# A mixture-of-experts kernel whose token rows for the third and later experts are gathered in three steps among the products of the expert before

## The chip, the cores and the metric

One core of one Trainium2 chip runs the whole program. The metric is device time in microseconds (us): the median of three runs. Besides, one execution was recorded by the hardware profiler; all rows below are from that one. A core has TensorE (PE; its weight loads are shown apart as PEld), VectorE (DVE), ScalarE (ACT), GpSimd (POOL), SyncE (SP) and 16 DMA engines. TensorE reads SBUF and writes PSUM; the other engines bring PSUM back into SBUF.

## The reference

One layer of a diffusion backbone on 512 tokens of 1024 columns: a mixer (attention, a Hyena and a convolution group, an output projection), then a mixture of 16 experts in which every expert picks its 64 tokens. All values are float32. What matters here is the second half:

```python
def expert_choice_ffn(h, w_router, w1, w3, w2):
    cap = EC_CAPACITY * L // N_EXPERTS
    aff = jax.nn.softmax((h @ w_router).astype(jnp.float32), axis=-1)
    gate, idx = lax.top_k(jnp.swapaxes(aff, 1, 2), cap)
    xe = h[b_idx, idx]
    a = jnp.einsum('becd,edf->becf', xe, w1)
    u = jnp.einsum('becd,edf->becf', xe, w3)
    y = jnp.einsum('becf,efd->becd', jax.nn.silu(a) * u, w2)
    y = y * gate[..., None].astype(y.dtype)
    return jnp.zeros_like(h).at[b_idx, idx].add(y)
...
h2 = modulate(rmsnorm(x, norm2_g[l]), sh2, sc2)
x = x + g2 * expert_choice_ffn(h2, router_w[l], expert_w1[l], expert_w3[l], expert_w2[l])
return rmsnorm(x, final_norm_g)
```

## The kernel before

The first 400 us hold the mixer and the routing; they end with `idxf`, the list of each expert's 64 token numbers. From there a loop over the 16 experts (line 1267 on) runs, one expert after the other. An expert's weights are 24 tiles of 128 x 2048 float32, 1 MB each: for each k of 8 one tile of w1 and one of w3, then eight tiles of w2. They are loaded by SyncE's queue, in the order of use, into a pool of 22 such tiles (`U`, tag "U"). Two of the 22 hold the running sums (`acc`) from expert 1 on and two the rows of x (`xblk`), so 18 are left for loads, 20 once the rows of x are given back. `take` asks for a loaded tile, `free` gives it back after its last product and issues the next load; each of these waits for the products that read its buffer, and for the load eight places ahead of it to land. A load is thus held up whenever TensorE stands still for long.

The steps of an expert, with their names: for each k, 8 products into four PSUM tiles `pa` (lines 1279 and 1280), with the expert's transposed token rows `xT[:, k, cs]` (64 columns) as the stationary side and the weight tile as the moving side of 512 columns. `xT` is half of the tile `xh` and holds two experts' columns side by side, 64 each. A float32 product shows as two records in the trace, a transpose as one. After every second k one piece of `scatter` of the preceding expert follows: two products `pZ` (line 1177) that add its rows `yg` onto the sums, with additions on VectorE (line 1180). Then VectorE and ScalarE copy `pa` to `au` (lines 103 and 105, in turn), 16 transposes bring it into `pT` (line 1307), ScalarE and VectorE make `hT` of it (1309, 1310), and 32 products `py` (line 1320) with the eight w2 tiles follow. VectorE scales the result into `yg` (line 1324).

The token rows come from `gather(i)`, which serves the two experts 2i and 2i+1 at once. TensorE broadcasts the two lists (`pB`, line 1155), VectorE compares them with the token numbers into `ohg`, one-hot columns times the token's norm factor (line 1159), and for each of eight blocks of columns TensorE multiplies four 128 x 128 blocks of x, as the stationary side, with four blocks of `ohg`, 128 moving columns each (line 1167), so that the result is already transposed. `modulate2` (lines 1060 and 1062, ScalarE and VectorE in turn) takes each block from PSUM into `xT` with scale and shift. `gather(0)` runs among the first products of expert 0. For each odd expert but the last the whole gather for the next two experts stands between its `pa` products and its 16 transposes.

TensorE's order in the loop is the order of the code (`manual_schedule` for PE); the queues of the other engines are set by a scheduler. PSUM tiles come from three pools: "A" (four, `pa`), "T" (two: `pT` and `pZ`) and "Y" (two: `pB`, `pG`, `py`). The last expert's own residual rows are gathered by `final_rows` (line 1225) with one-hot columns as the stationary side.

Of the kernel before, what the change touches and what calls it, by code (L numbers as in the profile page):

```python
# [21 lines left out]
E = 16  # L22
# [28 lines left out]
def hybrid_kernel(ctx: ExitStack, tc: tile.TileContext, a, out: bass.AP):  # L51
# [34 lines left out]
    def psT(name="psT"):  # L86
        return psum.tile([128, 512], FT, name=name, tag="T", bufs=2)
# [682 lines left out]
    def finish(*gens):  # L770
        for g in gens:
            for _ in g:
                pass
# [374 lines left out]
    nc.vector.tensor_tensor(idxf, bc(sel), rv(lf[1])[:, None, :].to_broadcast([16, 2, CAP]), op=OP.add)  # L1148
    nc.vector.tensor_tensor(vals, bc(lv[0]), rv(lv[1])[:, None, :].to_broadcast([16, 2, CAP]), op=OP.max)

    def gather(i):

        pb = psY("pB")
        for s in range(2):
            mm(pb[:, 64 * s:64 * s + 64], ident[0:16, 2 * i + s:2 * i + s + 1].to_broadcast([16, 128]), idxf[:, 0],
               start=True, stop=True)
        g = W("ohg")
        for b in range(4):
            nc.vector.tensor_scalar(g[:, 128 * b:128 * b + 128], pb[:, 0:128], tok[:, b:b + 1], rsT[:, b:b + 1],
                                    op0=OP.is_equal, op1=OP.mult)  # L1160
        yield
        for k in range(8):
            if k % 4 == 0 or i == 0:
                p = psT("pT")
            pk = p[:, (k % 4) * 128:(k % 4 + 1) * 128]
            for b in range(4):
                mm(pk, xblk(b)[:, k * 128:(k + 1) * 128], g[:, b * 128:(b + 1) * 128], start=(b == 0), stop=(b == 3))  # L1167
            modulate2(xT[:, k], pk, k)
            yield

    def scatter(e, yg, oh):

        def block(c):
            ps = [psT("pZ") for _ in range(2)]
            for h in range(2):
                pr = slice(64 * h, 64 * h + 64)
                mm(ps[h], oh[pr, 128 * c:128 * c + 128], yg[pr], start=True, stop=True)  # L1177
            for h in range(2):
                s = slice(512 * h, 512 * h + 512)
                nc.vector.tensor_add(ablk(c)[:, s], (ablk if e else xblk)(c)[:, s], ps[h])  # L1180
        return [lambda c=c: block(c) for c in range(4)]
# [10 lines left out]
    xhU = late.tile([128, 2048], FT, name="xh")  # L1192
    xT = half(xhU, 0).rearrange("p (k n) -> p k n", k=8)
    hT = half(xhU, 1).rearrange("p (f n) -> p f n", f=16)
    first = gather(0)
    in_order = ExitStack()
    in_order.enter_context(tc.manual_schedule(engines={mybir.EngineType.PE}))
    next(first)
# [68 lines left out]
    for e in range(E):  # L1267
# [4 lines left out]
            nc.vector.tensor_scalar(oh, iota, ig[:, e:e + 1], None, op0=OP.is_equal)  # L1272
        pa = [psA("pa") for _ in range(4)]
        back = deque(scatter(*prev)) if prev is not None else deque()
        for k in range(8):
            w1, w3 = take(("w1", e, k)), take(("w3", e, k))
            for f in range(4):
                s = slice(512 * f, 512 * f + 512)
                mm(pa[f][0:64], xT[:, k, cs], w1[:, s], start=(k == 0), stop=(k == 7))  # L1279
                mm(pa[f][64:128], xT[:, k, cs], w3[:, s], start=(k == 0), stop=(k == 7))  # L1280
                if e == 0 and f == 1:
                    next(first, None)
            free(2, 2 if e == 1 and k < 2 else 0)
            if k == 1 and e == 1:
                acc = [U("acc0"), U("acc1")]
            for _ in range(2 if last and k else int(k % 2 == 1)):
                if back:
                    back.popleft()()
            if last and k == 3:
                rows = final_rows()  # L1290
                bg = next(rows)
            if last and k == 5:
                fgh, pairs, where = next(rows)
                next(rows)
        assert not back
        au = [W("au") for _ in range(4)]
        for f in range(4):
            copy(au[f], pa[f])
        if e % 2 == 1 and e + 1 < E:
            finish(gather(e // 2 + 1))  # L1300
            if e + 3 == E:
                free_only(2)
        for f in range(4):
            p = psT("pT")
            for i in range(4):
# [137 lines left out]
```

## Time and profile before

| what | value |
|---|---|
| median of three runs | 1355.02 us (1353.71 to 1356.91) |
| the profiled execution | 1362.26 us, its span 1360.5 us |
| mean granted TensorE clock | 0.955 |
| TensorE busy | 1253.2 us (92%) |
| VectorE, ScalarE, GpSimd busy | 491.1, 213.1, 154.3 us |
| DMA | 458.01 MB, mean 337 GB/s over the span |
| pa products (lines 1279, 1280) | 2048 records, 596 ns each, two at a time |
| py products (line 1320) | 1024 records, 596 ns each, two at a time |
| gather products (line 1167) | 512 records, 363 ns each, 101.9 us busy |

The profile is read in this manner. Busy shares are of one execution, and are averages over stretches with different limits. The slices give the shares over time; windows give them for a stretch between two named moments, with the clock that TensorE was granted (1.00 is 2.4 GHz, 0.50 is 1.2 GHz) and the rate of the DMA engines. The timeline gives instructions in order, with the idle time before them and what ended it; rows of one kind are merged, so the second number is the stretch that all of them took together. What sets the time of a stretch is the wait in it that ends last.

### The profile page before, as it was taken

How to read it: one execution, taken by the hardware profiler on the slowest of the kernel's cores; microseconds unless marked ns; L12 is line 12 of the kernel's file. 1: busy time of each engine (PE TensorE's matmuls, PEld its weight loads, DVE VectorE, ACT ScalarE, POOL GpSimd, SP SyncE). 2: the span in 40 equal slices, each digit the busy share in tenths (PEclk: the TensorE clock that was granted, in tenths of full speed). 3: DMA queues.
4: the chain of work that ended last, by engine and by line, in shares of the span. 5: the costliest groups of instructions: out<-in, count | busy, mean ns of one | idle time of the engine just before them, and what ended most of it. 6: DMA issues, size and time to landing. Idle time of an engine off the chain costs nothing.

```text
span 1360.5 us, 15095 instructions
## 1 busy us (share of the span) xinstructions
PE 1253.2 (92%) x6084; PEld 614.1 (45%) x6084; DVE 491.1 (36%) x971; ACT 213.1 (16%) x445; POOL 154.3 (11%) x166
## 2 busy tenths in 40 slices
PE   5898988899979999998998999899899999989997
PEld 2576567766644344335334333533433353353332
DVE  6877998478580121211112122021211212121224
ACT  3532232245420100001000000000100000000002
POOL 1333444546110000000000000000000000000000
PEclk9998999999989989996999999799999989979998
DMA  9934124634367997999999999999999999999994
GB/s 354 354 135 170 67 66 113 216 136 171 126 247 317 421 422 289 422 421 407 421 422 421 421 420 422 421 422 421 422 420 422 421 421 421 421 421 421 422 421 189
DMA packets 72980, 458.01 MB, mean 337 GB/s; under 512 B 7364, under 2 KB 9228, under 8 KB 21710
## 3 DMA queue, kind: packets, MB, share of 16 engines
q1 hardware_dynamic: 71662, 453.64, 82.2%
q0 software_dynamic: 912, 3.06, 0.9%
q8 instruction: 48, 0.79, 0.2%
q10 hardware_dynamic: 336, 0.35, 0.1%
q14 instruction: 22, 0.18, 0.0%
HBM read 453.87 MB, written 2.36 MB: 335 GB/s over the span
## 4 chain that ended last, share of the span: by engine, by line
PE 65%; DMA 16%; DVE 15%; issue 2%; ACT 2%; POOLq 0%; DVEq 0%; SPq 0%; ACTq 0%
PE pa L1279 24%; DMA ld<-in_w_dram 15%; PE py L1320 12%; PE pT L1167 7%; DVE glu L590 4%; PE pZ L1177 4%; PE pT L1307 2%; PE pP L550 1%; PE pP L548 1%; PE pP L549 1%; PE pS L932 1%; PE pO L963 1%; PE pM L431 1%; PE pX L548 1%; PE pX L550 1%
## 5 line engine op out<-in xcount | busy, mean ns | idle before, releaser
L1280 PE MATMUL pa<-ld,xh 128*64 128x512 f32 x1024 | 455.9, 596 | 3.3 <-DMA ld<-in_w_dram 3.3
L1279 PE MATMUL pa<-ld,xh 128*64 128x512 f32 x1024 | 455.6, 596 | 0.3 <-DVE xh L1062 0.3
L1279 PEld LDWEIGHTS pa<-ld,xh 128*64 128x64 f32 x1024 | 135.7, 137 | 280.0 <-issue 267.9
L1320 PE MATMUL py<-ld,xh 128*64 128x512 f32 x1024 | 224.4, 596 | 0.0
L1180 DVE TENSOR_TENSOR acc<-acc,pZ 128x512 f32<-128x512 f32 x112 | 72.0, 684 | 296.7 <-PE pZ L1177 296.7
L1280 PEld LDWEIGHTS pa<-ld,xh 128*64 128x64 f32 x1024 | 135.6, 137 | 20.4 <-issue 12.9
L1320 PEld LDWEIGHTS py<-ld,xh 128*64 128x64 f32 x1024 | 72.3, 137 | 140.1 <-issue 135.5
L1167 PE MATMUL pT<-ohg,ld 128*128 128x128 f32 x512 | 101.9, 363 | 31.1 <-DVE xh L1062 15.1
L103 ACT ACTIVATE au<-pa 128x512 f32<-128x512 f32 x32 | 19.1, 597 | 632.3 <-PE pa L1280 632.3
L1167 PEld LDWEIGHTS pT<-ohg,ld 128*128 128x128 f32 x512 | 87.8, 257 | 49.6 <-DVE xh L1062 22.1
L1347 POOL DMA_INDIRECT out_dram<-yg,where x1 | 1.1, 1096 | 950.9 <-DVE yg L1346 950.9
L1324 DVE SCALAR_TENSOR_TENSOR yg<-py,ig,g1bc 128x512 f32<-128x512 f32 x16 | 12.0, 752 | 206.1 <-PE py L1320 206.1
L516 POOL TENSOR_TENSOR wl<-ld,wh 128x512 fp32r<-128x512 f32 x44 | 64.5, 1492 | 85.8 <-ACT wh L515 46.3
L1177 PE MATMUL pZ<-yg,oh 64*128 64x512 f32 x240 | 68.9, 641 | 1.5 <-DVE acc L1180 1.5
L548 PE MATMUL pP<-hh,wh 128*128 128x512 f32 x144 | 58.8, 409 | 1.2 <-ACT hh L505 1.2
L550 PE MATMUL pP<-hh,wl 128*128 128x512 f32 x144 | 57.2, 405 | 2.7 <-DVE wl L516 2.7
L549 PE MATMUL pP<-hl,wh 128*128 128x512 f32 x144 | 57.0, 397 | 1.5 <-DVE hl L507 1.5
L590 DVE SCALAR_TENSOR_TENSOR glu<-glu,p 128x512 f32<-128x512 f32 x60 | 56.9, 949 | 1.1
L1307 PE MATMUL pT<-c,au 128*128 128x128 f32 x256 | 46.0, 315 | 11.4 <-DVE acc L1180 5.4
L1062 DVE TENSOR_SCALAR xh<-pT,A,B 128x128 f32<-128x128 f32 x32 | 13.1, 410 | 112.1 <-PE pT L1167 112.1
L105 DVE COPY au<-pa 128x512 f32<-128x512 f32 x32 | 22.1, 692 | 74.1 <-PE pa L1280 72.0
L1307 PEld LDWEIGHTS pT<-c,au 128*128 128x128 f32 x256 | 36.9, 209 | 25.7 <-DVE acc L1180 11.2
(336 smaller groups left out, 1279.0 us busy)
## 6 DMA issues: line engine op xcount, KB each, us to landing
ld<-in_w_dram SPq DMA_DIRECT2D x384, 1024.0 KB, 19.8
ld<-in_w_mod_dram SPq DMA_DIRECT2D x24, 1024.0 KB, 13.5
ld<-in_w_in_dram SPq DMA_DIRECT2D x11, 1024.0 KB, 5.2
ld<-in_w_out_dram SPq DMA_DIRECT2D x4, 1024.0 KB, 5.3
ld<-in_x_dram SPq DMA_DIRECT2D x2, 1024.0 KB, 12.0
ld<-in_x_dram SPq DMA_DIRECT2D x4, 512.0 KB, 6.7
out_dram<-acc SPq DMA_DIRECT2D x4, 512.0 KB, 5.3
g<-in_rpb_dram POOLq DMA_DIRECT2D x8, 244.5 KB, 6.0
```

The lines of the kernel that those rows point to most:

```text
L516: (nc.vector if i in dve else nc.gpsimd).tensor_sub(lo[:, s], raw[:, s], hi[:, s].bitcast(FT))
L548: mm(ps, l[0], r[0], start=start, stop=False)
L549: mm(ps, l[0], r[1], start=False, stop=False)
L550: return mm(ps, l[1], r[0], start=False, stop=stop)
L590: nc.vector.scalar_tensor_tensor(yc[i], glt[i][:, j:j + 512], cw[:, i, j:j + 1], yc[i], op0=OP.mult, op1=OP.add)
L1167: mm(pk, xblk(b)[:, k * 128:(k + 1) * 128], g[:, b * 128:(b + 1) * 128], start=(b == 0), stop=(b == 3))
L1177: mm(ps[h], oh[pr, 128 * c:128 * c + 128], yg[pr], start=True, stop=True)
L1180: nc.vector.tensor_add(ablk(c)[:, s], (ablk if e else xblk)(c)[:, s], ps[h])
L1279: mm(pa[f][0:64], xT[:, k, cs], w1[:, s], start=(k == 0), stop=(k == 7))
L1280: mm(pa[f][64:128], xT[:, k, cs], w3[:, s], start=(k == 0), stop=(k == 7))
L1307: nc.tensor.transpose(p[:, i * 128:(i + 1) * 128], au[f][:, c:c + 255:2], ident)
L1320: mm(py[64 * h:64 * h + 64], hT[:, f], w2[:, i * 1024 + 512 * h:i * 1024 + 512 * h + 512], start=(f == 0), stop=(f == 15))
```

## The change

`gather` is split in two. `first_rows` is the old way, for experts 0 and 1 alone. `next_rows(e)` gathers the 64 rows of one expert e, from expert 2 on, in three steps: the list of one expert is broadcast and compared (four comparisons of 64 columns); then eight products of `ohg` (64 one-hot columns as the stationary side) with 512 columns of x as the moving side give the 64 rows in one PSUM tile `pG`, the columns' halves on partitions 0 to 63 and 64 to 127, copied to the new tile `xg`; then four transposes and eight `modulate2` of 64 columns write the expert's half of `xT`. In experts 1 to 14 these steps follow the products of k = 2, 4 and 6. The whole gather between the products and the transposes is gone. The two tiles of x rows are given back after the products of expert 14 instead of 13; no load is issued by that call.

```diff
@@ -1148,25 +1148,50 @@
     nc.vector.tensor_tensor(idxf, bc(sel), rv(lf[1])[:, None, :].to_broadcast([16, 2, CAP]), op=OP.add)
     nc.vector.tensor_tensor(vals, bc(lv[0]), rv(lv[1])[:, None, :].to_broadcast([16, 2, CAP]), op=OP.max)
 
-    def gather(i):
+    def first_rows():
 
         pb = psY("pB")
         for s in range(2):
-            mm(pb[:, 64 * s:64 * s + 64], ident[0:16, 2 * i + s:2 * i + s + 1].to_broadcast([16, 128]), idxf[:, 0],
-               start=True, stop=True)
+            mm(pb[:, 64 * s:64 * s + 64], ident[0:16, s:s + 1].to_broadcast([16, 128]), idxf[:, 0], start=True, stop=True)
         g = W("ohg")
         for b in range(4):
             nc.vector.tensor_scalar(g[:, 128 * b:128 * b + 128], pb[:, 0:128], tok[:, b:b + 1], rsT[:, b:b + 1],
                                     op0=OP.is_equal, op1=OP.mult)
         yield
         for k in range(8):
-            if k % 4 == 0 or i == 0:
-                p = psT("pT")
+            p = psT("pT")
             pk = p[:, (k % 4) * 128:(k % 4 + 1) * 128]
             for b in range(4):
                 mm(pk, xblk(b)[:, k * 128:(k + 1) * 128], g[:, b * 128:(b + 1) * 128], start=(b == 0), stop=(b == 3))
             modulate2(xT[:, k], pk, k)
             yield
+
+    def next_rows(e):
+
+
+        pb = psY("pB")
+        mm(pb[:, 0:64], ident[0:16, e:e + 1].to_broadcast([16, 128]), idxf[:, 0], start=True, stop=True)
+        g = W("ohg")
+        for b in range(4):
+            nc.vector.tensor_scalar(g[:, 64 * b:64 * b + 64], pb[:, 0:64], tok[:, b:b + 1], rsT[:, b:b + 1],
+                                    op0=OP.is_equal, op1=OP.mult)
+        yield
+        pg = psY("pG")
+        for b in range(4):
+            for h in range(2):
+                mm(pg[64 * h:64 * h + 64], g[:, 64 * b:64 * b + 64], xblk(b)[:, 512 * h:512 * h + 512],
+                   start=(b == 0), stop=(b == 3))
+        xg = W("xg")
+        copy(xg, pg)
+        yield
+        p = psT("pT")
+        c0 = 64 * (e % 2)
+        for c in range(4):
+            nc.tensor.transpose(p[:, 128 * c:128 * c + 128], xg[:, 128 * c:128 * c + 128], ident)
+        for c in range(4):
+            for h in range(2):
+                modulate2(xT[:, 4 * h + c, c0:c0 + 64], p[:, 128 * c + 64 * h:128 * c + 64 * h + 64], 4 * h + c)
+        yield
 
     def scatter(e, yg, oh):
 
@@ -1192,7 +1217,7 @@
     xhU = late.tile([128, 2048], FT, name="xh")
     xT = half(xhU, 0).rearrange("p (k n) -> p k n", k=8)
     hT = half(xhU, 1).rearrange("p (f n) -> p f n", f=16)
-    first = gather(0)
+    first = first_rows()
     in_order = ExitStack()
     in_order.enter_context(tc.manual_schedule(engines={mybir.EngineType.PE}))
     next(first)
@@ -1272,6 +1297,7 @@
             nc.vector.tensor_scalar(oh, iota, ig[:, e:e + 1], None, op0=OP.is_equal)
         pa = [psA("pa") for _ in range(4)]
         back = deque(scatter(*prev)) if prev is not None else deque()
+        rows = next_rows(e + 1) if 1 <= e < E - 1 else iter(())
         for k in range(8):
             w1, w3 = take(("w1", e, k)), take(("w3", e, k))
             for f in range(4):
@@ -1286,6 +1312,8 @@
             for _ in range(2 if last and k else int(k % 2 == 1)):
                 if back:
                     back.popleft()()
+            if not last and k in (2, 4, 6):
+                next(rows, None)
             if last and k == 3:
                 rows = final_rows()
                 bg = next(rows)
@@ -1296,10 +1324,8 @@
         au = [W("au") for _ in range(4)]
         for f in range(4):
             copy(au[f], pa[f])
-        if e % 2 == 1 and e + 1 < E:
-            finish(gather(e // 2 + 1))
-            if e + 3 == E:
-                free_only(2)
+        if e + 2 == E:
+            free_only(2)
         for f in range(4):
             p = psT("pT")
             for i in range(4):
```

On TensorE, at the end of an odd expert's products (`pa` and `pZ` as above, `pB` the broadcast list, `au` the copied products), the rows before are these:

```order
L1280 MATMUL pa<-ld,xh 64x512
L1177 MATMUL pZ<-yg,oh 128x512 x2
L1155 MATMUL pB<-p_70,c_72 128x64 x2
L1167 MATMUL pT<-ohg,ld 128x128 x32
L1307 MATMUL pT<-c_72,au 128x128 x16
L1320 MATMUL py<-ld,xh 64x512 x32
```

And the rows of the same expert with the change, from the products of k = 2 on; the lines of dots stand for the products of `pa`, eight for each k, between the rows:

```order
L1173 MATMUL pB<-p_70,c_72 128x64
...
L1202 MATMUL pZ<-yg,oh 128x512 x2
...
L1182 MATMUL pG<-ld,ohg 64x512 x8
...
L1202 MATMUL pZ<-yg,oh 128x512 x2
...
L1190 MATMUL pT<-c_72,xg 128x128 x4
...
L1202 MATMUL pZ<-yg,oh 128x512 x2
L1333 MATMUL pT<-c_72,au 128x128 x16
L1346 MATMUL py<-ld,xh 64x512 x32
```

The 32 products of 128 columns between the last scatter piece and the transposes have moved out; eight products and four transposes stand among the products of `pa`, the transposes eight products ahead of the last scatter piece.

On VectorE, at the same place of expert 1, before (`acc` the sums, `xh` the tile with `xT` and `hT`):

```order
L105 COPY au<-pa 128x512 [waits DVE_49,PE_49] x2
L1180 TENSOR_TENSOR acc_3528<-ld,pZ 128x512 [waits PE_49] x2
L1159 TENSOR_SCALAR ohg<-pB,c_72,rsT 128x128 [waits PE_49]
L1159 TENSOR_SCALAR ohg<-pB,c_72,rsT 128x128 x3
L1062 TENSOR_SCALAR xh<-pT,A_83,B_84 128x128 [waits PE_49]
L1062 TENSOR_SCALAR xh<-pT,A_83,B_84 128x128 [waits PE_49,Activation_49]
L1062 TENSOR_SCALAR xh<-pT,A_83,B_84 128x128 [waits PE_49]
L1062 TENSOR_SCALAR xh<-pT,A_83,B_84 128x128 [waits PE_49,Activation_49]
L1310 TENSOR_TENSOR xh<-xh,pT 128x256 [waits Activation_49] x4
```

And with the change:

```order
L1062 TENSOR_SCALAR xh<-pT,A_83,B_84 128x64 [waits Activation_49]
L105 COPY au<-pa 128x512 [waits PE_49]
L1062 TENSOR_SCALAR xh<-pT,A_83,B_84 128x64 [waits Activation_49]
L105 COPY au<-pa 128x512 [waits DVE_49,PE_49]
L1062 TENSOR_SCALAR xh<-pT,A_83,B_84 128x64 [waits Activation_49]
L1205 TENSOR_TENSOR acc_3528<-ld,pZ 128x512 [waits PE_49]
L1062 TENSOR_SCALAR xh<-pT,A_83,B_84 128x64 [waits Activation_49]
L1205 TENSOR_TENSOR acc_3528<-ld,pZ 128x512 [waits PE_49]
L1336 TENSOR_TENSOR xh<-xh,pT 128x256 [waits Activation_49] x4
```

The evacuations of the gathered rows have moved ahead of the copies of `pa` and the last additions, and alternate with them; each waits for ScalarE, which does the other half of them.

## Rows read from the trace of the kernel before

**Rows 1.** The page's part 2: busy tenths and GB/s in 40 equal slices of the span.

```profile
PE   5898988899979999998998999899899999989997
...
DMA  9934124634367997999999999999999999999994
...
GB/s 354 354 135 170 67 66 113 216 136 171 126 247 317 421 422 289 422 421 407 421 422 421 421 420 422 421 422 421 422 420 422 421 421 421 421 421 421 422 421 189
```

**Rows 2.** Windows of 10 us: start:end, length, each engine's busy time (instructions), TensorE's clock, DMA.

```profile
core 0: us, PE busy (x) PEld busy (x) DVE busy (x) ACT busy (x) POOL busy (x), PEclk, DMA share, GB/s
...
510.00:520.00 10.00, 8.10 (x51) 5.72 (x52) 2.51 (x6) 2.46 (x6) 0.00 (x0) 0.98 0.13 56
...
520.00:530.00 10.00, 10.00 (x50) 3.39 (x48) 0.00 (x0) 0.00 (x0) 0.00 (x0) 1.00 0.90 334
...
530.00:540.00 10.00, 10.00 (x48) 3.05 (x44) 1.14 (x2) 0.00 (x0) 0.00 (x0) 1.00 1.01 427
...
640.00:650.00 10.00, 10.00 (x48) 3.30 (x46) 0.00 (x0) 0.00 (x0) 0.00 (x0) 1.00 0.97 368
```

**Rows 3.** Windows from one expert's py to the next: 1 to 2, 2 to 3, 4 to 5, 12 to 13.

```profile
518.20:568.10 49.90, 48.86 (x227) 16.86 (x226) 9.19 (x17) 2.73 (x6) 0.00 (x0) 1.00 0.95 390
...
568.10:638.60 70.50, 65.95 (x295) 31.90 (x296) 12.45 (x25) 4.56 (x11) 0.00 (x0) 0.85 1.01 421
...
688.50:751.70 63.20, 58.57 (x294) 25.13 (x296) 12.39 (x25) 4.55 (x10) 0.00 (x0) 1.00 1.01 421
...
1154.80:1229.10 74.30, 68.01 (x295) 34.31 (x294) 12.31 (x25) 4.57 (x10) 0.00 (x0) 0.86 1.01 421
```

**Rows 4.** The page's part 6: DMA issues, count, KB each, median us from issue to landing.

```profile
ld<-in_w_dram SPq DMA_DIRECT2D x384, 1024.0 KB, 19.8
```

**Rows 5.** Waits of SyncE's queue, 420 to 560 us: total, times, longest.

```profile
SPq L162 <- PE py L1320: 48.1, 16, 23.0
```

**Rows 6.** Timeline around the gather after expert 1's products: start, us, engine, instructions.

```profile
496.17 1.13 PE L1177 MATMUL pZ<-yg,oh 64*128 64x512 f32 x4
...
501.10 2.08 PE L1167 MATMUL pT<-ohg,ld 128*128 128x128 f32 x8 [0.51 <-DVE xh L1062]
...
512.38 1.16 PE L1167 MATMUL pT<-ohg,ld 128*128 128x128 f32 x8 [0.55 <-ACT xh L1060]
...
518.17 2.37 PE L1320 MATMUL py<-ld,xh 128*64 128x512 f32 x10
```

**Rows 7.** Timeline, expert 14's way to py without a gather, and the last expert's py.

```profile
1274.04 1.13 PE L1177 MATMUL pZ<-yg,oh 64*128 64x512 f32 x4
...
1275.95 1.40 PE L1307 MATMUL pT<-c,au 128*128 128x128 f32 x8 [0.78 <-DVE acc L1180]
...
1278.96 13.95 PE L1320 MATMUL py<-ld,xh 128*64 128x512 f32 x64
...
1337.06 13.95 PE L1320 MATMUL py<-ld,xh 128*64 128x512 f32 x64
```

**Rows 8.** The window of 10 us in which the last load lands.

```profile
1330.00:1340.00 10.00, 9.55 (x52) 4.28 (x48) 7.54 (x20) 4.98 (x14) 0.00 (x0) 1.00 0.72 278
```

**Rows 9.** Timeline, the last expert's own rows: broadcast of the list, products with one-hot columns.

```profile
1313.98 0.43 PE L1218 MATMUL pB<-p,c 16*128 16x64 f32 x2
...
1314.79 3.65 PE L1225 MATMUL pG<-acc,ohg 128*64 128x512 f32 x16 [0.38 <-DVE ohg L1221]
```

**Rows 10.** Groups by line: shapes, count, busy us, mean ns, idle before: evacuations and copies.

```profile
L105 DVE COPY au<-pa 128x512 f32<-128x512 f32 x32 | 22.1, 692 | 74.1 <-PE pa L1280 72.0 <-PE pa L1279 2.0
...
L1060 ACT ACTIVATE xh<-pT,B,A 128x128 f32<-128x128 f32 x32 | 14.6, 458 | 164.0 <-PE pT L1167 164.0
...
L1062 DVE TENSOR_SCALAR xh<-pT,A,B 128x128 f32<-128x128 f32 x32 | 13.1, 410 | 112.1 <-PE pT L1167 112.1
```

**Rows 11.** TensorE's waits for loads, 880 to 1205 us, and a window in that stretch.

```profile
PE pa L1280 <- DMA ld<-in_w_dram: 3.3, 4, 0.9
...
1060.00:1080.00 20.00, 18.40 (x77) 7.15 (x75) 2.57 (x4) 0.00 (x0) 0.00 (x0) 1.00 1.01 421
```

## The prediction

> **What bounds the kernel now.** I read the page's slices first: in the last two thirds of the span both TensorE and the DMA engines stand at nine tenths, and the loads run at 421 GB/s in nearly every slice [rows 1]. Busy shares can't tell which of two full engines sets the end, so I read the stretches next. The experts read 384 loads of 1024 KB [rows 4]; one load is 1.0486 MB / 421 GB/s = 2.49 us, the 24 loads of an expert 59.8 us. TensorE's own period, from one expert's second product (py) to the next, is 49.9 us where no gather lies in it, and 63 to 74 us where one does, at a mean granted clock of 0.85, 1.00 and 0.86 in the three rows shown [rows 3]. Two experts cost it 113 to 124 us, against 119.6 us of loads. So the two run neck and neck, and small stalls of one become stalls of the other.
>
> The stalls show in two places. First, the gather for experts 2 and 3 (after expert 1's first products): pZ, the last scatter piece, begins at 496.17, the first py at 518.17, 22.0 us later [rows 6]; without a gather the same way takes 1278.96 - 1274.04 = 4.9 us [rows 7]. No weight tile is released in those 22 us, SyncE's next load waits up to 23.0 us for py [rows 5], all tiles are full, and the DMA runs dry: 56 GB/s in one 10-us row and 334 in the next [rows 2]. The hole is (421-56)/421 x 10 + (421-334)/421 x 10 = 8.7 + 2.1 = 10.8 us; the gather of expert 3 leaves another (421-368)/421 x 10 = 1.3 us [rows 2]. The rows after run slightly over 421, so I count 11.9 us in all. Second, the end: the last load lands at about 1330 + 278/421 x 10 = 1336.6 [rows 8], but py of the last expert only ends at 1337.06 + 13.95 = 1351.0 [rows 7], 14.4 us later. TensorE is late there because of the late gather for experts 14 and 15 (the 74.3-us period [rows 3]). After py come 9.5 us to the span's end at 1360.5.
>
> **What the change takes away.** The gathers of experts 2 to 15, seven blocks between the first products and the transposes of an odd expert. Beyond a plain period they cost TensorE 63.2 - 49.9 = 13.3, 70.5 - 49.9 = 20.6 and 74.3 - 49.9 = 24.4 us in the rows shown, the last with waits for loads in it [rows 3]; the first one 22.0 - 4.9 = 17.1 [rows 6, 7]. The gather that feeds experts 0 and 1 stays as it is.
>
> **What it adds**, for each of experts 1 to 14, c us of TensorE. The broadcast pB: the same shape took 0.43 [rows 9]. The eight products pG, 64 one-hot columns stationary and 512 moving: line 1225 already does exactly this for the last expert's rows, 3.65 us [rows 9]. Four transposes: eight of the same size took 1.40, so 0.70 [rows 7]. Sum 4.8. The waits in between are covered: 16 products, some 7 us, stand between pB and pG and again between pG and the transposes, while VectorE or ScalarE makes the one-hot columns and a copy. Not covered is the last step. The eight evacuations of pT stand right before the end of the first products, each waits for the other engine, and the copies of pa queue between them on VectorE and ScalarE. Half of the last scatter piece needs pT's PSUM buffer. The two sizes of row are 0.41 and 0.46 for 128 columns [rows 10]; with 64 columns they are no dearer, so the chain is at most 8 x 0.5 = 4 us, with the two copies of each engine (0.69 and less [rows 10]) up to 6.6. It starts 3.4 us before the last product ends (the eight products of the last pair of tiles, 16 records at 13.95/64 us each [rows 7]). Uncovered at most 6.6 - 3.4 = 3.2; at least about 0.2, since the transposes of au waited on additions there anyway [rows 7]. I take 1.0, near the lower end, since most of the chain runs beside the last eight products. So c is 5.0 to 8.0, taken as **5.8**, and the period 55.7 us, under the 59.8 us of loads. VectorE and ScalarE have the room: they are busy for 9.2 and 2.7 us of a plain period [rows 3]. The two tiles of x rows come free one expert later, so two loads may be issued later; TensorE by then waits for the loads in flight, not for tiles, so I cost it at nothing; without that cover it would be two loads, 5 us.
>
> **The sum.** From then on the loads set the pace. The DMA ran dry at 510 + 56/421 x 10 = 511.3 and resumed at 522.1, about 2.2 us after py's first tile came free (518.17 + 13.95/8 = 519.9). With the change py of expert 1 begins at 496.17 + 4.9 + c = 506.9, its first tile is free at 508.6, loads resume by 510.8, just before the DMA is dry; c over 6.3 would leave a hole of c - 6.3. So both holes close and the last load lands at 1336.6 - 11.9 = **1324.7**. The first pair of the last expert's loads is in 22 loads earlier, at 1324.7 - 54.8 = 1269.9. TensorE is waiting by then: first products of expert 15 could begin, by TensorE alone, at 501.1 + 13 x 49.9 + 13.4 + 14c = 1163.2 + 14c, which is 1244 for c = 5.8. The last expert's own work isn't touched: from its first product, 1292.3 (about py's end of 1279 + 13.4 [rows 7]), to py's end at 1351.0 are 58.7 us; it waits once more for the second pair (5.0 us of loads against 3.4 of products), 1.6 us, and then has extra scatter and output work that keeps it behind the loads. It ends at 1269.9 + 58.7 + 1.6 = 1330.2, where the last load needs it only after 1324.7. That is 20.8 us before 1351.0. I give back 0.5 us for the thin margin of the first hole: **20.3 us**. The profiled execution's 1360.5 us would become 1340.2; the median of the runs, 1355.02, was 7 us below the profiled time (1362.26), and the difference carries over: 1355.0 - 20.3 = **1334.7**.
>
> The rule that speaks against it: before the change TensorE waited for loads only a few times, 3.3 us in all between 880 and 1205, and the granted clock was 1.00 in a stretch where it did [rows 11]. After it, TensorE waits some 4 us in each expert from expert 8 or 9 on (first products by TensorE alone at 910, the loads for them in by 911, at expert 9), a little before every tile. The Trainium skill, "TensorE: Matmul & The Clock Gate", section "HAM oscillation — how this bites in real kernels", says that a DMA wait between groups of products can put the clock back to half each time. The row with waits does not bear it out, though its waits were rarer than those to come; if it held, the rival below gives the time.
>
> **Rivals.**
> 1. TensorE stays the bound. For c over (1269.9 - 1163.2)/14 = 7.6 TensorE never catches up with the loads, and each further 0.1 us costs 1.4 us. At c = 8.4 the first product of the last expert begins at 1280.8, 10.9 us later than forecast, with no wait for the second pair: 1344. For it: the ping-pong of evacuations. Against: 4.8 of c are measured shapes, and my bound for the rest ends at 8.0, where the last py would end at 1163.2 + 112 + 58.7 = 1333.9 and the time be 1338. Chance 9%.
> 2. The clock drops in the waits for loads. At half clock a pair of tiles takes 6.9 us of products instead of 3.4, against 5.0 of loads, so TensorE falls behind by 1.9 us a pair until it is back. Slack of 4 us an expert takes most of that up; what counts is a drop within the last expert, 3.4 to 7 us: 1338 to 1342. Chance 9%.
> 3. Slower: the new steps themselves bring the clock down, as the old gather did, where eight records of L1167 took 2.08 at the low clock and 1.16 at full [rows 6]. If half clock held for 10 us in every expert, c would be 5.8 + 5 = 10.8; the change breaks even at c = (1292.3 - 1163.2)/14 = 9.2, and 1.6 us over it, 14 times, is 22 us slower: 1377. Against: pG and the transposes ran at full clock at the end of the span, and the old gather fell to half where short products alternated with half-microsecond waits. Chance 4%.
> 4. It doesn't do what it says: the scheduler's queues on VectorE hold a step so that TensorE waits as long as the gather took, c near 9: no change, 1352 to 1358. Chance 3%.
>
> **How the numbers follow.** Forecast 75%, of 1330 to 1338. Its lower end is the floor of the loads: last load 1324.7, its products 1.7, the 9.5 us behind: 1335.9 of span, 24.6 us saved. The upper end is a hole of 1 to 2 us and a little clock. Rivals 1 and 2 reach from 1338 to 1352; I take the range to 1344, which leaves out the slow half of rival 1 and the last two. Faster by over 0.2% (2.7 us, about what a measurement of this kernel can tell from no change) 92%, within it 3%, slower 5%.
>
> **What would show it.** Right: no row under 415 GB/s from 430 us to the last load; that load at about 1325; periods of 55 to 56 us in experts 2 to 7 and of 59.8 later, with TensorE's waits for loads at 4 us each; pG at 3.65 us. Wrong: a hole after expert 1, an idle of over 3 us before the last scatter piece or the transposes of au (rival 1), granted clock under 1.00 inside the first products (rivals 2 and 3), or py of the last expert ending more than 8 us after the last load.

## The result, and the profile after

The changed kernel takes **1342.64 us** (median of five runs, 1341.67 to 1345.3) beside 1356.91 (1353.71 to 1364.36) of the kernel before in the same comparison: a ratio of 0.9893, 95% interval 0.9859 to 0.9927. The forecast was 1334.7 with a range of 1330 to 1344. The profiled execution of the changed kernel took 1341.92 us, its span 1340.1; the forecast of that span was 1340.2. So the span came out as worked out, the median 8 us above, and a gain of 14.3 us was measured where 20.3 were forecast. Both halves of that need an explanation.

First the page of after: the clock and the rate in 40 slices, the chain that ended last, and the groups of the new products, of the products that wait for loads, and of the new transposes.

```profile
PEclk9998999989989999999999999999999999999999
...
GB/s 344 375 138 162 77 63 118 190 127 185 139 270 276 421 422 421 422 421 421 421 420 420 422 421 421 421 421 421 421 421 421 422 421 421 421 421 422 421 420 256
...
PE 49%; DMA 35%; DVE 13%; issue 2%; ACT 1%; POOLq 0%; SPq 0%; DVEq 0%; ACTq 0%
...
L1306 PE MATMUL pa<-ld,xh 128*64 128x512 f32 x1024 | 463.8, 597 | 14.7 <-DMA ld<-in_w_dram 14.7
...
L1182 PE MATMUL pG<-ld,ohg 128*64 128x512 f32 x224 | 52.8, 592 | 0.0
...
L1190 PE MATMUL pT<-c,xg 128*128 128x128 f32 x56 | 9.2, 286 | 0.0
```

Where [rows 1] had a slice at 289 and one at 407, every slice from the fourteenth to the last but one now stands at 420 to 422. The new products and transposes have no idle time in front of them at all. In the chain that ended last one expert's new products stand with the time that they hold TensorE up:

```profile
703.95 3.43 PE pG L1182 x16
```

The windows that answer to [rows 2] (three of 10 us) and to [rows 3] (from py of expert 0 to the next, expert 2 to 3, expert 12 to 13); columns as there:

```profile
510.00:520.00 10.00, 10.00 (x49) 3.31 (x47) 1.15 (x2) 0.00 (x0) 0.00 (x0) 1.00 1.01 419
520.00:530.00 10.00, 10.00 (x48) 3.27 (x46) 2.39 (x6) 0.00 (x0) 0.00 (x0) 1.00 1.02 420
...
640.00:650.00 10.00, 10.00 (x47) 3.29 (x46) 2.39 (x6) 0.00 (x0) 0.00 (x0) 1.00 1.01 422
```

```profile
446.60:502.40 55.80, 54.73 (x249) 18.80 (x248) 12.70 (x26) 4.13 (x10) 0.00 (x0) 1.00 1.01 421
...
558.20:614.80 56.60, 55.64 (x249) 19.39 (x248) 12.40 (x26) 4.13 (x10) 0.00 (x0) 0.97 1.02 422
...
1135.10:1195.60 60.50, 58.23 (x249) 22.77 (x248) 12.46 (x26) 4.13 (x10) 0.00 (x0) 1.00 1.01 421
```

The holes after expert 1 (56 and 334 GB/s before) and after expert 3 (368) are gone. Up to py of expert 7 the periods are 55.1 to 55.8, one of them 56.6 with 3.4 us of half clock in it; from there on 59.5 to 60.9, the pace of the loads. The way to py at the end of expert 1's products, where 22.0 us stood in [rows 6], and the waits of SyncE's queue from 420 to 560 us ([rows 5]):

```profile
492.03 0.66 PE L1190 MATMUL pT<-c,xg 128*128 128x128 f32 x4
...
496.20 1.12 PE L1202 MATMUL pZ<-yg,oh 64*128 64x512 f32 x2
...
498.10 1.12 PE L1202 MATMUL pZ<-yg,oh 64*128 64x512 f32 x2 [0.78 <-DVE acc L1205]
499.15 3.27 PE L1333 MATMUL pT<-c,au 128*128 128x128 f32 x16
...
502.35 1.08 PE L1346 MATMUL py<-ld,xh 128*64 128x512 f32 x4
```

```profile
SPq L162 <- PE pa L1306: 79.1, 22, 6.0
SPq L162 <- PE py L1346: 30.6, 16, 7.2
```

From the last scatter piece to py are 6.2 us with one wait of 0.78, and the queue's longest wait for py is 7.2 instead of 23.0. Lastly TensorE in the last expert (the wait for the second pair of tiles, py), which answers to [rows 7]:

```profile
1269.76 1.02 PE L1305 MATMUL pa<-ld,xh 128*64 128x512 f32 x2
1271.00 0.64 PE L1306 MATMUL pa<-ld,xh 128*64 128x512 f32 x1 [0.22 <-DMA ld<-in_w_dram]
...
1275.97 0.64 PE L1306 MATMUL pa<-ld,xh 128*64 128x512 f32 x1 [1.32 <-DMA ld<-in_w_dram]
```

```profile
1316.91 13.95 PE L1346 MATMUL py<-ld,xh 128*64 128x512 f32 x64
```

py of the last expert ends at 1330.9 (1351.0 before), and 9.3 us follow to the end.

### The profile page after: what moved, and what is told of

It reads as the page before. It is cut to its first block, busy times and chain, and to the rows that moved or that the text cites. A ratio compares the mean times of both kernels' runs of the same rounds, so it can differ in the third digit from the quotient of the medians.

```text
span 1340.1 us, 14779 instructions
## 1 busy us (share of the span) xinstructions
PE 1255.4 (94%) x5916; PEld 578.9 (43%) x5916; DVE 505.7 (38%) x1034; ACT 223.9 (17%) x480; POOL 156.5 (12%) x166
## 4 chain that ended last, share of the span: by engine, by line
PE 49%; DMA 35%; DVE 13%; issue 2%; ACT 1%; POOLq 0%; SPq 0%; DVEq 0%; ACTq 0%
DMA ld<-in_w_dram 33%; PE pa L1305 18%; PE py L1346 7%; DVE glu L590 4%; PE pZ L1202 3%; PE pG L1182 2%; PE pP L550 1%; PE pP L548 1%; PE pP L549 1%; PE pS L932 1%; PE pO L963 1%; PE pM L431 1%; PE pX L548 1%; PE pX L549 1%; PE pX L550 1%
## 5 line engine op out<-in xcount | busy, mean ns | idle before, releaser
L1306 PE MATMUL pa<-ld,xh 128*64 128x512 f32 x1024 | 463.8, 597 | 14.7 <-DMA ld<-in_w_dram 14.7
L1305 PE MATMUL pa<-ld,xh 128*64 128x512 f32 x1024 | 466.4, 597 | 0.3 <-DVE xh L1062 0.3
L1305 PEld LDWEIGHTS pa<-ld,xh 128*64 128x64 f32 x1024 | 131.6, 136 | 199.1 <-issue 191.2
L1306 PEld LDWEIGHTS pa<-ld,xh 128*64 128x64 f32 x1024 | 132.2, 137 | 102.5 <-issue 65.1
L1060 ACT ACTIVATE xh<-pT,B,A 128x64 f32<-128x64 f32 (+1 forms) x60 | 24.4, 406 | 443.1 <-PE pT L1190 334.3
L1202 PE MATMUL pZ<-yg,oh 64*128 64x512 f32 x240 | 84.4, 640 | 4.8 <-DVE acc L1205 3.9
L1182 PE MATMUL pG<-ld,ohg 128*64 128x512 f32 x224 | 52.8, 592 | 0.0
L1202 PEld LDWEIGHTS pZ<-yg,oh 64*128 64x128 f32 x240 | 22.7, 184 | 65.6 <-issue 35.7
L103 ACT ACTIVATE xg<-pG 128x512 f32<-128x512 f32 x7 | 4.2, 597 | 279.3 <-PE pG L1182 279.3
L1062 DVE TENSOR_SCALAR xh<-pT,A,B 128x64 f32<-128x64 f32 (+1 forms) x60 | 20.7, 344 | 73.5 <-ACT xh L1060 28.5
(345 smaller groups left out, 1353.7 us busy)
## 6 DMA issues: line engine op xcount, KB each, us to landing
ld<-in_w_dram SPq DMA_DIRECT2D x384, 1024.0 KB, 19.8
```

Of the source, the lines that this page charges most:

```text
L1182: mm(pg[64 * h:64 * h + 64], g[:, 64 * b:64 * b + 64], xblk(b)[:, 512 * h:512 * h + 512], start=(b == 0), stop=(b == 3))
```

## The experiments

Theory: after the change the loads set the end, TensorE's added work is free below some 7.6 us an expert, and the gain is the closed hole plus TensorE's lateness in the last expert. Rivals: TensorE still sets the end, so that each us of its work counts; or the gain hangs on one place or on the new form, not on the spreading. Experiments 1 to 8 edit the changed kernel, 9 to 11 edit nothing. Each ratio is to the kernel before on the same chip (medians 1357.1 for experiments 1 to 4, 1357.5 for 5 to 8); c is TensorE's added work in an expert, as in the prediction.

**1. No gather at all for experts 2 to 15.**

```diff
-        rows = next_rows(e + 1) if 1 <= e < E - 1 else iter(())
+        rows = iter(())
```

> The changed kernel without any gather for experts 2 to 15: the eight products, the transposes and their evacuations are left out, and the later experts work on the rows of experts 0 and 1. TensorE loses about 5.4 us in each of 14 experts. Theory 1, the loads set the pace and TensorE has slack: span 1338 to 1342 us (the changed kernel: 1340.1), timed 1339 to 1345, with longer waits of TensorE for loads. Theory 2, TensorE's own work sets the pace and the gain came from less of it: 14 x 5.4 = 75 us less, about 1265.

Measured: 1342.22 us (1340.88 to 1342.59), 0.9892 (0.9876 to 0.9909), the same as the changed kernel. The chain and TensorE's waits from 440 us on:

```profile
DMA 52%; PE 32%; DVE 13%; issue 2%; ACT 1%; POOLq 0%; SPq 0%; DVEq 0%; ACTq 0%
```

```profile
PE pa L1306 <- DMA ld<-in_w_dram: 58.0, 56, 1.4
```

TensorE is done 5 us earlier in each expert and waits for loads from expert 4 on (periods of 59.6 to 60.8) instead of 8. The new steps, all of them, cost nothing now, and less work for TensorE in experts 1 to 14 gains nothing more.

**2. One load in 24 left out** (from expert 1 on).

```diff
-        for j in range(8):
+        for j in range(8 if e == 0 else 7):
...
-            w2 = take(("w2", e, j))
+            w2 = take(("w2", e, j)) if e == 0 or j < 7 else w2
...
-            free(1, 0)
+            if e == 0 or j != 6:
+                free(1, 0)
```

> The changed kernel with 23 loads an expert instead of 24 from expert 1 on: the last w2 tile isn't read, its products use the tile before it. TensorE's work is the same, the load stream is 15 x 2.49 = 37 us shorter. Theory 1 (loads set the pace): TensorE takes over as the bound, first py of expert 1 at 502.4 + 13 periods of 55.4 + 13.4 + 58.7 + 9.5 = 1304; span 1302 to 1308. Theory 2 (TensorE sets it already): no change, 1340.

Measured: 1312.66 us (1311.9 to 1313.52), 0.9679 (0.9663 to 0.9695). The chain:

```profile
PE 80%; DVE 14%; issue 2%; DMA 2%; ACT 1%; POOLq 0%; DVEq 0%; ACTq 0%
```

30.0 us less than the changed kernel, with no wait for loads and periods of 55.1 to 56.7: here TensorE sets the end. The span is 1310.2, 6 us more than the 1304 that I had worked out and 2 over my range: py of expert 1 begins 4.4 us later (506.8 for 502.4), and the 13 periods after it are 1.9 us longer in all, three of them with 3.4 us of half clock. So in the changed kernel the loads alone hold 30 us that TensorE doesn't need.

**3. The new products twice**, the other side: TensorE's added work over the point of 7.6 us.

```diff
-        for b in range(4):
-            for h in range(2):
-                mm(pg[64 * h:64 * h + 64], g[:, 64 * b:64 * b + 64], xblk(b)[:, 512 * h:512 * h + 512],
-                   start=(b == 0), stop=(b == 3))
+        for again in range(2):
+            for b in range(4):
+                for h in range(2):
+                    mm(pg[64 * h:64 * h + 64], g[:, 64 * b:64 * b + 64], xblk(b)[:, 512 * h:512 * h + 512],
+                       start=(b == 0), stop=(b == 3))
```

> The changed kernel with the eight products pG done twice, 3.43 us more of TensorE in each of experts 1 to 14; nothing else changes. Theory 1 (slack of some 4 us an expert, a period of 58.8 against 59.8 of loads): TensorE's lag from the start no longer runs out, first product of the last expert at 502.4 + 3.4 + 13 x 58.8 + 13.4 = 1283.6 instead of 1269.8; span about 1352, no hole in the loads after expert 1 over 3 us. Theory 2 (TensorE sets the pace throughout): 14 x 3.43 = 48 us more, 1388. Clock rival: if such products bring the clock down, granted clock under 0.95 in the periods and more than 1360.

Measured: 1369.82 us (1368.46 to 1370.56), 1.0100 (1.0084 to 1.0117): slower than before. Periods are 59.2 and 60.0 in turn, so c is 9.3 to 10.1, mean 9.7; every second one holds 3.4 us of half clock. My 1352 took 8.9 (periods of 58.8) and full clock. With 9.7 the prediction's own formula gives 1163.2 + 14 x 9.7 + 58.7 + 9.5 = 1367.2 for the span; it was 1366.7. My clock rival asked for more than 1360 and a granted clock under 0.95 in the periods; the time is over that, but the clock is 0.97 and more, and the half clock costs 0.8 us in every second period. Besides, the hole is back:

```profile
500.00:510.00 10.00, 9.22 (x38) 4.26 (x36) 4.78 (x10) 3.73 (x9) 0.00 (x0) 0.83 0.93 376
510.00:520.00 10.00, 10.00 (x50) 3.41 (x48) 0.42 (x1) 0.00 (x0) 0.00 (x0) 1.00 0.84 318
```

That is (421-376)/421 x 10 + (421-318)/421 x 10 = 3.5 us; the prediction's c - 6.3 gives 3.4.

The first three agree with one picture: flat up to some point, then 14 us for each us of c, and by that formula slower than before from c of about 9. The slope itself rests on this point and, with a wider miss, on the next.

**4. The three steps in one block**, where the old gather stood.

```diff
-            if not last and k in (2, 4, 6):
-                next(rows, None)
...
+        if not last:
+            finish(rows)
```

> The new form at the old place: for experts 1 to 14 the three steps stand in one block between the products and the transposes of au, instead of after k = 2, 4 and 6. Theory 1, the place is what counts: with its waits bare the block takes about 10 us (broadcast and comparisons 2, products 3.4, copy and transposes 1.5, evacuations 3.3), period 60 us, a hole in the loads of some 4 us after expert 1, TensorE behind the loads at the end: span 1360 to 1375. Rival, the form is what counts (512 moving columns instead of 128): 1340 to 1346.

Measured: 1347.52 us (1344.61 to 1351.91), 0.9927 (0.9910 to 0.9944). TensorE's waits:

```profile
PE pT L1333 <- DVE xh L1336: 30.0, 30, 1.8
PE pG L1182 <- DVE ohg L1176: 17.7, 14, 1.3
PE pT L1190 <- DVE xg L105: 5.6, 7, 0.8
PE pT L1190 <- ACT xg L103: 4.9, 7, 0.7
```

The last three are 28.2 us of waits in 14 gathers, 2.0 each, that the spreading hides (experiment 1, on the same chip, took 1342.22). The first is as much again: in the block the transposes of au wait behind the evacuations of the gathered rows. In the changed kernel that line stands with 2.2 us. Periods are 57.6 to 59 (one of 60.6), c about 8 and not the 10 that I had expected: just over the point, so the time lies between my two forecasts and meets neither. With 8.2, the mean of the periods, the formula gives 1346.2 for the span; it was 1350.1. The hole after expert 1 is one row of 333 GB/s, 2.1 us. Of the 14 us of the change, then, about 9 come with the new form in one place, and spreading it brings the other 5.

**5. The old form spread** over the products of the odd experts, one block after each k.

```diff
-        rows = next_rows(e + 1) if 1 <= e < E - 1 else iter(())
+        rows = gather(e // 2 + 1) if e % 2 == 1 and not last else iter(())
...
-            if not last and k in (2, 4, 6):
+            if not last:
                 next(rows, None)
```

> The old form at the new place: each odd expert up to 13 gathers for both next experts with x as the stationary side and 128 moving columns, one block of columns after the products of each k. Theory 1 (the place counts): about 9.8 us of TensorE per pair of experts at full clock against 9.6 of the new form, so 1340 to 1345 of span, with up to 3.5 us of hole after expert 1. Rival (the form counts, by the clock or by its waits): 16.6 us and more a pair, granted clock under 0.95 in the odd experts' periods, 1347 to 1356.

Measured: 1350.47 us (1344.84 to 1350.54), 0.9936 (0.9914 to 0.9958). Up to expert 7 odd periods take 62.5, even ones 49.9, so a pair costs 112.4, hardly more than the 110.9 of the changed kernel, and no half clock stands in the later gathers. Yet expert 1 bears the work of two experts before the loads have any slack, and the hole is half there:

```profile
500.00:510.00 10.00, 9.23 (x50) 4.12 (x46) 3.08 (x5) 1.30 (x3) 0.00 (x0) 1.00 0.81 307
510.00:520.00 10.00, 9.68 (x49) 4.23 (x49) 1.68 (x4) 1.84 (x5) 0.00 (x0) 1.00 0.81 290
```

(421-307)/421 x 10 + (421-290)/421 x 10 = 5.8 us, and it took 8 us more than the changed kernel, above the 1340 to 1345 that I had expected. What closes the hole, then, is a share of the work in each period, one expert at a time; that is argued, since the old form for one expert at a time was not run.

**6 and 7. The new form for experts 2 and 3 only, or for 14 and 15 only**; the others keep the old one.

```diff
+    NEW = (2, 3)
...
-        rows = next_rows(e + 1) if 1 <= e < E - 1 else iter(())
+        rows = next_rows(e + 1) if e + 1 in NEW else iter(())
...
+        if e % 2 == 1 and e + 1 < E and e + 1 not in NEW:
+            finish(gather(e // 2 + 1))
```

> The change for experts 2 and 3 alone; experts 4 to 15 get their rows by the old gather, in pairs, at the old place. Theory 1 (two separate gains): the hole in the loads after expert 1 is gone (no 10-us row under 415 GB/s between 500 and 530), TensorE is as late as before at the end; about 10.6 us less than the kernel before: span near 1350 by the profiled one, timed near 1346. Rival (one gain, all of it at the end): no change, 1357.

Measured: 1349.01 us (1346.93 to 1354.01; four of seven up to 1349.0, three from 1353.8), 0.9955 (0.9929 to 0.9981). The first hole is nearly closed (rows of 411 and 397), but the next old gather, for experts 4 and 5, now opens one:

```profile
630.00:640.00 10.00, 9.93 (x47) 4.07 (x48) 1.48 (x4) 1.15 (x3) 0.00 (x0) 0.89 0.46 165
```

That is 6.1 us, where the same gather left 1.3 before. In these runs the hole stands where a long gather first meets loads that have run ahead to the last free tile.

> The change for experts 14 and 15 alone; experts 2 to 13 by the old gather. Theory 1: the hole after expert 1 stays (a row near 56 GB/s), the last expert is bound by the loads again, as in the changed kernel, but 12 us later: about 5.6 us less than before, timed near 1351, py of the last expert ends 9 to 10 us after the last load instead of 14. Rival (the hole is all): no change, 1357; or 20 us less, 1337, if the end is all.

Measured: 1355.67 us (1352.24 to 1358.88), 0.9983 (0.9964 to 1.0002): no difference that can be told. The hole is as before:

```profile
510.00:520.00 10.00, 8.61 (x52) 5.92 (x54) 2.09 (x5) 2.45 (x6) 0.00 (x0) 1.00 0.09 38
```

Experts 12 to 15 follow the loads (periods of 56.2, 60.4, 61.8), py of the last begins at 1330.8. The last load lands at 1339.5 and py ends at 1344.8, 5.3 us after it. TensorE's lateness at the end is gone, but the loads are as late as ever: alone it is worth 2 us by the medians, which can't be told from nothing, and not the 6 I had expected. Why stands with experiment 9.

**8. Less work in the last expert**: the broadcast of the final gain (line 1259) moved into expert 14, the last scatter one piece after each of k = 0 to 3.

```diff
-            for _ in range(2 if last and k else int(k % 2 == 1)):
+            for _ in range(int(k < 4) if last else int(k % 2 == 1)):
...
-            if last and k == 3:
+            if last and k == 4:
...
             free_only(2)
+            final_gain()
```

> The changed kernel with less work in the last expert: the broadcast of the final gain moves into expert 14, and the last scatter goes one piece after each of k = 0 to 3 instead of two after k = 1 and 2; the residual rows follow k = 4. Theory 1 (loads set the pace up to the last expert's first tiles, and from there its own work on TensorE sets the end): 2.0 us of broadcast and 2 x 0.8 of waits less, span about 1336.5. Rival (the last load sets the end): no change, 1340.

Measured: 1342.22 us (1340.60 to 1343.62), 0.9888 (0.9866 to 0.9910): no gain over the changed kernel. py begins at 1316.69, as there, but now its last eight records wait for the last load:

```profile
1316.69 12.24 PE L1352 MATMUL py<-ld,xh 128*64 128x512 f32 x56
1329.35 1.94 PE L1352 MATMUL py<-ld,xh 128*64 128x512 f32 x8 [0.42 <-DMA ld<-in_w_dram]
```

TensorE and the last load now end together. Yet this profile isn't level with that of the changed kernel: its loads ran later (the last is issued at 1309.54, there at 1305.79), and its span is only 0.5 us longer. Measured from the landing of the last load, py of the last expert ends after 2.0 us instead of 5.3. So the lighter last expert gave some 3 us here, near the 3.6 that I had expected, but it is one profile, and the medians don't show it. No version that does all the work beats the changed kernel by more than its runs differ.

**9 to 11. Both kernels profiled again**, unchanged, since the profiled pair differed by 20.3 us and the medians by 14.3.

> The kernel before as it is, profiled a second time. Theory (the gathers of before fall to half clock by different amounts in each execution): in the first profile five of seven gathers stood at half clock for 10 to 20 us each, 78.5 us in all, and the execution took 1362; this one differs from it mainly there: its time goes with the sum of half clock in the gathers of experts 3 to 13, some 55 us of it for an execution of 1355 and the last py at about 1330, and everything up to expert 0's py lies within 4 us of the first profile (450.1). Rival (the spread comes from before the experts, or from the loads): the same half clock in the same gathers, and a py of expert 0 or a rate of the loads that makes up the difference.

> The kernel before, profiled a third time; the same two theories as for the second. If the gathers' half clock decides, the three profiles order by time as they order by the half clock of the gathers, and a gather that stood at half clock in one profile runs at full clock (a period of 63.2 us) in another.

> The changed kernel, profiled a second time. Theory: the half-clock stretches of 3.4 us at 408 and 449 us, which stood in the first profile of before and not in that of after, come and go from execution to execution with either kernel; where they stand, py of expert 0 begins near 450 instead of 446.5, the loads run some 3 us later throughout, and the execution takes 1344 to 1345 instead of 1342. Rival: they belong to the kernel before alone; then py of expert 0 begins at 446.5 again and the time is 1342.

Measured: before 1355.52 and 1361.65 us, after 1346.57. The stretch with the last gather (experts 14 and 15) in the first, the second and the third profile of before, one row each:

```profile
1195.00:1230.00 35.00, 29.50 (x126) 20.77 (x126) 8.34 (x18) 4.57 (x10) 0.00 (x0) 0.71 1.01 422
```

```profile
1195.00:1230.00 35.00, 29.53 (x160) 16.39 (x158) 7.68 (x17) 4.56 (x10) 0.00 (x0) 1.00 1.01 421
```

```profile
1195.00:1230.00 35.00, 29.65 (x127) 20.74 (x125) 7.83 (x17) 4.56 (x10) 0.00 (x0) 0.71 1.01 422
```

The first two agree up to py of expert 12 (1154.74 and 1154.66). Then the last gather runs at half clock in the one and at full clock in the other: 74.3 against 66.5 us to the next py, the last py at 1337.06 against 1330.49, spans of 1360.5 and 1353.7. In the third it is at half clock again: 1336.46 and 1359.8. I had expected the sum of half clock in all gathers to order the three; it doesn't (78.5, 58.0 and 85.4 us of it, for 1362.3, 1355.5 and 1361.7). The third has its half clock in the gather at 970 us where the others have it at 1087, and is within 2.1 us of them at py of expert 12. The last gather tells them apart.

In the second profile the last load and the last py stand so:

```profile
1319.40 0.33 SPq L162 DMA_DIRECT2D ld<-in_w_dram  x1
...
1330.49 13.95 PE L1320 MATMUL py<-ld,xh 128*64 128x512 f32 x64
```

That load took 20.5 us and lands at 1339.9, so py ends 4.6 us after it; in the first profile it lands at 1339.1 and py ends 11.9 us after it, in the changed kernel 5.3. In an execution whose last gather keeps the full clock there is no lateness at the end to take away. The change for experts 14 and 15 alone (span 1354.1) accordingly gained nothing beside the second profile (1353.7).

The row in which the experts' loads pick up, in the first profile of before, in that of after, and in the second of after:

```profile
410.00:420.00 10.00, 10.00 (x50) 4.37 (x48) 0.41 (x1) 0.46 (x1) 0.00 (x0) 0.93 0.50 179
```

```profile
410.00:420.00 10.00, 10.00 (x54) 4.30 (x52) 0.41 (x1) 0.46 (x1) 0.00 (x0) 1.00 0.79 296
```

```profile
410.00:420.00 10.00, 10.00 (x46) 4.06 (x44) 0.95 (x6) 0.46 (x1) 0.00 (x0) 0.86 0.32 115
```

3.4 us at half clock at 409 and again at 450 us stand in the second profile, as in all three of before. py of expert 0 begins at 451.8 instead of 446.5, py of the last at 1321.0 instead of 1316.9. A start that is some 4 us later stays so to the end, 4.7 us in the time. The half clock at 409 us is not all of it: the first load of expert weights is issued at 293.92 us in the second and at 290.95 in the first, so 3.0 us were lost before. That difference belongs to the executions, not to the change.

## Why the forecast was right, and where not

**The range: met, but in part by luck.** 1342.6 lies above 1330 to 1338, to which I gave 75%, and inside the range only by the part that I had added for rivals 1 and 2. Neither came: c stayed under 7.6, and the clock fell in no wait for loads. What put the time there was another thing, told at the end of this section.

**The bound and the hole: right.** The rate never falls under 416 GB/s in a row from 430 to 1310 us, and experiments 1 and 2 show that the loads set the pace; the last 5.3 us behind the last load are TensorE's own work in the last expert. The two loads that I costed at nothing cost nothing: every slice but the last stands at 420 and more to the end. The margin was as thin as said: in the later start of the second profile one row fell to 410, 0.3 us.

**The cost c = 5.8: right.** 55.1 to 55.8 less 49.9 is 5.2 to 5.9. The parts: pG 3.43 us for 3.65, the transposes 0.66 for 0.70. What I bounded by 0.2 and 3.2 and took as 1.0 is read from the way between the last scatter piece and py: 6.15 us in experts 1 and 2 (above), 5.4 to 5.7 from expert 4 on, beside 4.9 without a gather, so 1.2 and then 0.5 to 0.8. In experts 1 to 3 the second half of the scatter piece waits 0.78 us for VectorE's addition of the first, which stands between two evacuations there.

**Where TensorE meets the loads: right**, at expert 8, as worked out. The wait for the second pair in the last expert was 1.32 for 1.6. The waits before it are shorter than the 4 us an expert that I gave as a sign: 14.7 us in 16 waits. The rest of the longer periods counts as busy, 58.2 us beside 54.7 for the same 249 records in the windows above: a product whose partner's tile isn't there yet runs alone (two records in 1.02 us at 1269.76) and not two at a time.

**The clock rival: fell.** The granted clock is 1.00 in the stretch of 1135 to 1196 us, where TensorE waits before its tiles, and in nearly every other row. In experiment 1 it is 1.00 too, with 56 waits. The rule of the Trainium skill ("TensorE: Matmul & The Clock Gate", section "HAM oscillation — how this bites in real kernels") has for its example a kernel that waits longer for each slice than it computes on it; here the waits are 1.3 us at the longest beside 3.4 us of products for a pair of tiles, and no run tests it with longer ones.

**Rivals 1, 3 and 4: none came; the price of 1 and 3 holds in one run.** c stayed under 7.6, and no wait of TensorE at the new steps is over 0.8 us. Experiment 3, at c of 9.7, ends 0.5 us from the formula, and is slower than before, as a break-even point of 9.2 asks.

**The span of 1340.2: misses that cancel.** I let the last load of before land where the bytes run out at 421 GB/s, at 1336.6. The trace shows when it was issued, and how long it alone took to land:

```profile
1319.36 0.33 SPq L162 DMA_DIRECT2D ld<-in_w_dram  x1
...
ld<-in_w_dram SPq DMA_DIRECT2D x1, 1024.0 KB, 19.8
```

It lands at 1339.1, 2.5 us later than I took it. This is the rate of before from 1320 us in steps of 1 us:

```profile
DMA  9999999999999765541999999500000000000240
GB/s 401 426 426 418 434 426 410 426 418 418 426 418 418 328 279 238 221 205 41 209 311 373 381 324 295 209 12 0 0 0 0 0 0 0 0 0 0 94 168 0
```

From 1333 on the rate falls step by step while the last loads are still to land (what follows 1339 is the output). In the changed kernel the last load is issued at 1305.79 and lands at 1325.6, for 1324.7 forecast, 13.5 us earlier than in before. Of these, (296-179)/421 x 10 = 2.8 us are an earlier start of that execution, by the row of 410 to 420; the closed holes brought the other 10.7, and not the 11.9 that I had counted. So 2.5 and 1.2 us too late and 2.8 too early came to 0.9. In the second profile, whose start is later than that of before by (179-115)/421 x 10 = 1.5 us, the last load is issued at 1309.93 and lands at 1329.7, 9.4 us earlier than in before: 10.9 for the holes, and a span of 1344.3. That the first profile came so near to 1340.2 is luck.

**The step that failed: "the difference carries over".** Of the 20.3 us that I subtracted from the median, about 6.6 were the half clock of before's last gather, which the first profile had and an execution of 1355.5 hasn't. The new end doesn't depend on it: it goes by the loads and by the last expert's own work. So the end of the sum could be worked out from that profile, but the saving could not be taken off a median: an execution of 1355 had already lost less. What should have been subtracted from 1355.0 is 20.3 - 6.6 = 13.7, which gives 1341.3; the medians differ by 14.3. The hint was there: 7 us between the profiled time and the median, and two stretches of half clock in [rows 3]. In 24 further executions of before (1351.6 to 1362.2) time and mean clock go together, with a correlation of -0.78. That the other executions differ by the same gather is argued from three profiles, not shown for each, and it can't be all: the times of experiment 7, whose last gather is the new one, spread from 1352.2 to 1358.9. What spreads those stays open.

## What to carry to other kernels

Where the new end is set by a stream that the change doesn't touch, forecast the end itself, not a saving; and before carrying a saving from a profile to a median, ask which part of it that execution alone may have had. Where loads and an engine run neck and neck, work that is spread evenly over the loads' periods is free up to the difference, and the same work in one place is not. A stall of TensorE made a hole in the loads here only where they had run ahead to the last free tile, so look for the first one, and for the next that takes its place once it is gone; removing the last alone brought nothing that could be told.

## What the hardware showed beside

The last load of a long stream isn't complete when its bytes at the full rate would be through: here the rate fell from 421 GB/s to 205 over the last 6 us, and the last load landed 2.5 us after that count, 19.8 us after its issue like the median of all loads [rows 4]. The clock fell for 3.4 us at a time at the same two places, 408 and 449 us, in some executions and not in others of one kernel, and for 10 to 20 us in the old gather, in a different set of its seven places each time. The Trainium skill ("TensorE: Matmul & The Clock Gate", section "A second HAM failure mode: psum-queue depth-cycling") says that frequent short idles between groups of products can make the clock swing, which agrees with the old gather's waits of half a microsecond [rows 6]; that they are the cause no run here shows, since two or three of the seven gathers kept the full clock in each profile. With the new products and transposes, spread among the others, one such stretch of 3.4 us stands in the 14 periods of either profile of the changed kernel, and with twice the products one in every second period.
